# A first projection over successive tokens, and what is moved into its time, in a Hymba-style block on one Trainium2 core

## The chip, the core and the metric

The kernel runs on one core of one Trainium2 chip. The core has a matrix engine (TensorE, PE in the rows of the profile, with the weight loads apart as PEld), a vector engine (VectorE, DVE), a scalar engine (ScalarE, ACT), GpSimd (POOL) and SyncE (SP), which in this kernel issues nearly all DMAs. Each engine works through its own queue in order and waits on semaphores for the others. The metric is the device time of one execution in microseconds (us): 2374.28 us before the change, the median of 3 runs (2373.72 to 2376.62).

## What is computed

One layer of a streaming encoder trunk, batch 1, 2048 tokens of 1024 features, all float32. One RMSNorm feeds one projection, whose columns go to two mixers; both outputs are normalised, joined, projected and added to the input; a SwiGLU feed-forward layer follows. In short:

```python
h = rmsnorm(x, norm_mix_g)
u, q, k, v = split(h @ w_in)                  # 512 columns for u, 3 * 512 for q, k, v
# mixer A: 32 groups of 16 channels, one 64-state complex diagonal SSM per group
lam_bar = exp(lam * dt); b_bar = ((lam_bar - 1) / lam)[..., None] * b
s_t = lam_bar * s_{t-1} + b_bar u_t           # over the 2048 tokens
ya = gelu(Re(c s_t) + d * u_t); ya = ya * sigmoid(ya @ w_glu + b_glu)
# mixer B: 8 heads of 64, each chunk of 64 tokens sees itself and 8 chunks before it
yb = softmax(q k^T / 8 + rel_bias) v
x = x + concat(rmsnorm(ya), rmsnorm(yb)) @ w_out
x = x + (silu(hf @ w_gate) * (hf @ w_up)) @ w_down,  hf = rmsnorm(x)
out = rmsnorm(x)
```

## The kernel before, in words

Every product of float32 matrices is made of three matmuls (`mm3`, the matmul itself at L75): each operand is split into a high part (a cast on ACT) and a low part (a subtraction on DVE or POOL), and high times high, low times high and high times low are added up in PSUM. The PE's instructions stay in the order in which the program writes them (`Ordered`, `keep_in_program_order`); the order on the other engines and on SP's queue is set by a scheduler that goes by priorities, and is fixed when the program is built.

**First projection** (`u_phase`, L388 to 500). It makes `u`, 512 features by 2048 tokens, in four blocks `b` of 512 tokens. The tokens are taken by residue: token t is 8c + j, and a block holds two residues j with all 256 values of c, from an input `xp` that lies in that order. A block is four groups `f` of 128 features, each a sum over the inner dimension of 1024 in eight tiles `q`. Block 0 runs with q outermost over four PSUM banks, so it can follow its operands as they arrive; blocks 1 to 3 run group by group (`group`), each group through all q. `prep` loads and splits the operands of a block, `sums` loads the tokens again for the sums of squares and makes their inverse roots on DVE (`newton`, 14 small operations on 128x4), `spread_` turns these on the PE into a factor per token (tile `pb`), and `evac` (L448, tile `us`) multiplies the PSUM banks with it on DVE and stores the result to `u` in DRAM, laid out `[512, 8, 256]`: channel, residue, c. Between blocks `step` runs pieces of `ssm_prologue` (L155 to 386), which makes the SSM's matrices from its parameters: powers `pr`, `pi` (DVE), the powers `a8` (POOL), the products `v` and `wt` of powers with C and B (`cmul`, L280 to 282; DVE), `kt`, and transposes `bst` on the PE.

**Attention and SSM** (`att_phase`, from L620). `hT_unit(0)` loads the first 512 tokens (`xt`, 8 DMAs), scales them and splits them into `hi` and `lo` (L663 to 665), the operands of the first q, k and v products (`pf`). Then 128 steps follow, in which score blocks `sc`, transposes `pt` and products with v run, and between them pieces of eight `ssm_unit`s (L497 to 595), 64 channels each. A unit starts every 15 steps. It loads its `U` (128 x 4 x 256: residue and channel of the group by group by c) from `u`, and its matrices `Bst`, `Tm` and `Vm`; the PE first makes `pj<-U,Bst` (8 passes), POOL and DVE run the recurrence, and at the end the PE makes `pj<-U,Tm` and the rest of the output, which 8 DMAs store as `y`. `U` has one buffer, so the loads of a unit wait for the last read by the unit before it. The loads of a unit are issued from L506:

```python
for j in range(L):
    load(U[j * CH : (j + 1) * CH], S["u"][b * F : (b + 1) * F, j, :].rearrange("(g c) t -> c g t", c=CH))
```

Each of the 8 is 16 partitions by 4 groups by 256 values of c, 64 KB in runs of 1024 bytes. They all go through SP's queue, as do the stores of `y` and the other loads of the attention.

After the attention come the output projection (`mix`), the feed-forward layer (`gate_up`, `down`) and the last norm, which the change doesn't touch.

Of the kernel before, what the change touches and what calls it, by code (L numbers as in the profile page):

```python
# [13 lines left out]
ALU = mybir.AluOpType  # L14
# [29 lines left out]
PRO = 5  # L44
# [110 lines left out]
def ssm_prologue(k, ident, S):  # L155
# [3 lines left out]
    with tc.tile_pool(name="pro", bufs=1) as p:  # L159
# [158 lines left out]
        extend(pr, pi, 4, 4)  # L318
        a8 = S["a8"]
# [12 lines left out]
        def pc(a, qs, n):  # L332
            return a[:, qs, :n].unsqueeze(3).to_broadcast([P, 4, n, CH])

        def rc(a, qs):
            return a[:, qs, L - 1 :: -1].unsqueeze(3).to_broadcast([P, 4, L, CH])

        def cc(a, qs, n):
            return a[:, qs].unsqueeze(2).to_broadcast([P, 4, n, CH])

        for g2 in range(2):
            for c, bt in ((0, bbr), (1, bbi)):
                nc.gpsimd.dma_start(S["bb"][:, g2, c].rearrange("q n m -> n q m"), bt[g2 * NS : (g2 + 1) * NS])
        wts = []
        for b_ in range(4):
            qs = slice(4 * b_, 4 * b_ + 4)
            vt = [k.t(p, f"v{i}", [P, 4, 9, CH], bufs=2) for i in range(2)]
            cmul(vt[0][:], vt[1][:], pc(pr, qs, 9), pc(pi, qs, 9), cc(cr, qs, 9), cc(ci, qs, 9), [4, 9, CH], neg=True)
            for g2 in range(2):
                for c in range(2):  # L350
                    nc.gpsimd.dma_start(S["v"][qs, g2, c].rearrange("q n m -> n q m"),
                                      vt[c][g2 * NS : (g2 + 1) * NS].rearrange("n q k c -> n q (k c)"))
            if b_:
                yield
        for b_ in range(4):
            qs = slice(4 * b_, 4 * b_ + 4)
            wt = [k.t(p, f"wt{i}", [P, 4, L, CH], bufs=4) for i in range(2)]
            cmul(wt[0][:], wt[1][:], rc(pr, qs), rc(pi, qs), cc(bbr, qs, L), cc(bbi, qs, L), [4, L, CH])
            wts.append(wt)
        kt = k.t(p, "kt", [CH, 8, P], bufs=2)  # L360
        nc.gpsimd.memset(kt[:], 0.0)
        for b_ in range(4):
            nc.gpsimd.dma_start(S["kt"][:, 8 * b_ : 8 * b_ + 8, 0], kt[:])
        bb = k.t(p, "bbg", [P, NG, CH])
        nc.sync.dma_start(bb[:], S["bb"].rearrange("q g c n m -> (c n) (q g) m"))
        dm = k.t(p, "dm", [CH, NG, CH])
        V.tensor_tensor(dm[:], ident[:CH, :CH].unsqueeze(1).to_broadcast([CH, NG, CH]),
                        ddt[:].unsqueeze(2).to_broadcast([CH, NG, CH]), op=ALU.mult)
        vgs = []
        for b_ in range(4):  # L370
            vgs.append(k.t(p, "vg" if b_ < 2 else "bst", [P, 8, P], bufs=2))
            nc.sync.dma_start(vgs[b_][:], S["v"].rearrange("q g c n m -> (c n) (q g) m")[:, 8 * b_ : 8 * b_ + 8, :P])
        for b_ in range(4):
            gs = slice(8 * b_, 8 * b_ + 8)
            vg = vgs[b_]
            kt = k.t(p, "kt", [CH, 8, P], bufs=2)
            if b_ == 0:
                yield
# [6 lines left out]
            V.tensor_tensor(kt[:, :, :CH], kt[:, :, :CH], dm[:, gs], op=ALU.add)  # L385
            nc.gpsimd.dma_start(S["kt"][:, gs, 1], kt[:])
# [4 lines left out]
def u_phase(k, ident, S):  # L391

    tc, nc, io = k.tc, k.nc, k.io
    with ExitStack() as cx:
        p2 = cx.enter_context(tc.tile_pool(name="u2", side="right", bufs=2))
        p1 = cx.enter_context(tc.tile_pool(name="u1", side="right", bufs=1))
        p3 = cx.enter_context(tc.tile_pool(name="u3", side="right", bufs=4))
        psum = cx.enter_context(tc.tile_pool(name="ups", bufs=6, space=bass.MemoryType.PSUM, reuse_waits="tile"))
        psum2 = cx.enter_context(tc.tile_pool(name="ups2", bufs=2, space=bass.MemoryType.PSUM, reuse_waits="tile"))
        k.pro_psum = psum2  # L400
        wh, wl = k.t(p1, "wuh", [P, KT, DS], F32R), k.t(p1, "wul", [P, KT, DS], F32R)
        rsn = S["rsn"][:].rearrange("p (c j) -> p j c", j=L)
        te = k.te
        X, ST, pbs = {}, {}, {}

        def prep(b, each=None):
            X[b] = []
            for q in range(KT):
                if b == 0:
                    if q % 2 == 0:  # L410
                        xn = k.t(p2, "xn", [P, D], bufs=3)
                    raw = xn[:, q % 2 * DS : q % 2 * DS + DS]
                    nc.sync.dma_start(raw, io["w_u"][q * P : (q + 1) * P, :])
                    nc.scalar.activation(wh[:, q, :], raw, AF.Copy, scale=k.gm[:, q : q + 1])
                    nc.vector.scalar_tensor_tensor(wl[:, q, :], raw, k.gm[:, q : q + 1], f32(wh[:, q, :]),
                                                   op0=ALU.mult, op1=ALU.subtract)
                xt = k.t(p3, "xt", [P, 512])
                nc.sync.dma_start(xt[:], io["xp"][q * P : (q + 1) * P, 2 * b : 2 * b + 2, :].rearrange("p j c -> p (j c)"))
                hi, lo = k.t(p2, f"hi{q}", [P, 512], F32R), k.t(p2, f"lo{q}", [P, 512], F32R)
                nc.scalar.copy(hi[:], xt[:])  # L420
                nc.vector.tensor_tensor(lo[:], xt[:], f32(hi[:]), op=ALU.subtract)
                X[b].append((hi, lo))
                if each:
                    each(q)
            ST[b] = ss = k.t(p2, "ss", [P, 4])
            for i in range(4):
                xn = k.t(p2, "xn", [P, D], bufs=3)
                nc.sync.dma_start(xn[:], io["x"].rearrange("(h p j) d -> j h p d", p=P, j=L)[2 * b + i // 2, i % 2])
                nc.scalar.activation(xn[:], xn[:], AF.Square, accum_out=ss[:, i : i + 1])

        def mm(b, f, ps, q):
            fs = slice(f * P, (f + 1) * P)
            mm3(te, ps[:], wh[:, q, fs], wl[:, q, fs], X[b][q][0][:], X[b][q][1][:], q == 0, q == KT - 1)

        def sums(b):
            with tc.high_priority():
                ST[b] = newton(k, p2, ST[b][:], D, 4)

        def spread_(b):
            ps = k.t(psum2, "pp", [P, 512])  # L440
            spread(k, te, ps, ST[b], 0)
            pbs[b] = pb = k.t(p1, "pb", [P, 512])
            nc.scalar.copy(pb[:], ps[:])
            nc.scalar.copy(rsn[:, 2 * b : 2 * b + 2, :], pb[:].rearrange("p (j c) -> p j c", j=2))

        def evac(b, f, ps):
            us = k.t(p3, "us", [P, 2, NC], bufs=2)
            nc.vector.tensor_tensor(us[:], ps[:].rearrange("p (j c) -> p j c", j=2), pbs[b][:].rearrange("p (j c) -> p j c", j=2), op=ALU.mult)  # L448
            nc.sync.dma_start(S["u"][f * P : (f + 1) * P, 2 * b : 2 * b + 2, :], us[:])

        def group(b, f):
            ps = k.t(psum, "ps", [P, 512])
            for q in range(KT):
                mm(b, f, ps, q)
            return ps

        def finish(b, pss):
            with tc.high_priority():
                spread_(b)
                for f in range(4):  # L460
                    evac(b, f, pss[f])

        pss = [k.t(psum, "ps", [P, 512]) for _ in range(4)]

        def first(q):
            for f in range(4):
                mm(0, f, pss[f], q)
# [3 lines left out]
        def step(late=0):  # L471
            with tc.high_priority(offset=-late):
                next(pro)

        next(pro)
        prep(0, first)
        step(LATER)
        sums(0)
        held = pss
        for b in range(1, 4):  # L480
            prep(b)
            step()
            if b == 2:
                corner = k.t(p1, "corner", [64, 64])
# [4 lines left out]
            now = [group(b, 0)]  # L489
            finish(b - 1, held)  # L490
            now += [group(b, 1), group(b, 2)]
            sums(b)
            held = now + [group(b, 3)]
        step()
        finish(3, held)
# [3 lines left out]
def ssm_unit(k, p, psum, S, b, eng):  # L499
# [10 lines left out]
    for j in range(L):  # L510
        load(U[j * CH : (j + 1) * CH], S["u"][b * F : (b + 1) * F, j, :].rearrange("(g c) t -> c g t", c=CH))
# [108 lines left out]
def att_phase(k, ident, S, pro):  # L620
    tc, nc, io = k.tc, k.nc, k.io
    with ExitStack() as cx:
        aw = tc.alloc_tile_pool(name="aw", reuse_waits="tile", bufs=1, side="right")
        pfs = cx.enter_context(tc.tile_pool(name="apf", bufs=2, space=bass.MemoryType.PSUM, reuse_waits="tile"))
# [1003 lines left out]
```

## Time and profile before

| what | value |
|---|---|
| median of 3 runs | 2374.28 us (2373.72 to 2376.62) |
| span of the profiled execution, first to last instruction | 2370.8 us |
| PE busy | 2212.0 us (93%) |
| DVE, ACT, POOL busy | 1475.0, 1002.4, 1128.4 us (62, 42, 48%) |
| mean granted clock of the PE | 0.965 |
| first scores of the attention on the PE | at 178.83 us |
| loads of `U` | 64 DMAs of 64 KB, first issue at 192.9 us, last at 683.2 us |

The profiled execution is shown by its span alone; no time of its own is given beside it, so what lies around the span is seen only from the runs: their median is 3.5 us above it. A row of the timeline reads: start and duration in us, engine, line, operation, tile written <- tiles read, shape, and in brackets how long the engine stood idle before it and what released it. `SPq` rows are DMA issues on SP's queue: their duration is that of the issue, not of the transfer.

### The profile page before, as it was taken

The numbers are of one execution on the slowest core, as the hardware profiler recorded it, in microseconds if no ns is written. First come the engines' busy times: TensorE is split into PE (matmuls) and PEld (weight loads), VectorE is DVE, ScalarE is ACT, GpSimd is POOL, SyncE is SP. The second block draws the span as 40 slices with busy tenths as digits, with TensorE's granted clock in tenths as the row PEclk, the third lists the DMA queues.
The fourth block names the chain that finished last, engine by engine and source line by source line (L and its number), as shares of the span: only waits on it lengthen the run. The fifth ranks groups of instructions, "written<-read, shape, count | busy, mean of one in ns | idle before, by whom it ended". The sixth has DMA issues, their size and how long they took to land.

```text
span 2370.8 us, 30760 instructions
## 1 busy us (share of the span) xinstructions
PE 2212.0 (93%) x10712; PEld 1860.2 (78%) x10712; DVE 1475.0 (62%) x2247; ACT 1002.4 (42%) x1675; POOL 1128.4 (48%) x1268
## 2 busy tenths in 40 slices
PE   8588889999997899989999999999999989999996
PEld 6467778898986788768888887788888868888886
DVE  7644555756555855755776767766745365578675
ACT  5144545555556642243333334433333343345332
POOL 2313545656442333375555557655555464345442
PEclk9788999999998999989999999999999989999998
DMA  8587776766655334752544546654523187565541
GB/s 270 174 287 247 230 220 182 245 199 198 184 150 158 129 120 146 251 168 92 204 156 155 200 165 241 212 191 156 180 87 123 61 315 258 176 207 185 207 173 72
DMA packets 215220, 437.02 MB, mean 184 GB/s; under 512 B 27225, under 2 KB 57993, under 8 KB 207961
## 3 DMA queue, kind: packets, MB, share of 16 engines
q1 hardware_dynamic: 211480, 425.08, 54.1%
q0 software_dynamic: 3584, 9.98, 1.5%
q8 instruction: 84, 1.38, 0.2%
q14 instruction: 72, 0.58, 0.1%
HBM read 294.98 MB, written 132.15 MB: 180 GB/s over the span
## 4 chain that ended last, share of the span: by engine, by line
PE 50%; DVE 3%; issue 1%; POOL 1%; DMA 1%; ACT 1%; DVEq 0%; SPq 0%; ACTq 0%; POOLq 0%
PE X L75 19%; PE ps L75 17%; PE Y L75 10%; PE W L75 5%; DVE sa L1476 1%; DVE lo L152 1%; POOL c L152 0%; DVE hd L152 0%; DMA hd<-wc 0%; DVE S L1295 0%; DVE acc L1493 0%; DMA hd<-hq 0%; DVE g L1360 0%; DMA lo<-hc 0%; ACT hd L151 0%
## 5 line engine op out<-in xcount | busy, mean ns | idle before, releaser
L75 PE MATMUL X<-hi,c 128*128 128x512 f32 x1408 | 451.3, 391 | 8.0 <-ACT c L151 3.3
L75 PE MATMUL ps<-hd,hd 128*128 128x512 f32 (+1 forms) x1968 | 435.0, 384 | 7.7 <-DVE hd L152 4.6
L75 PEld LDWEIGHTS ps<-hd,hd 128*128 128x128 f32 x1968 | 361.5, 191 | 79.9 <-DVE hd L152 5.1
L152 POOL TENSOR_TENSOR c<-S,c 128x512 fp32r<-128x512 f32 x176 | 250.8, 1426 | 244.8 <-ACT c L151 242.9
L75 PEld LDWEIGHTS X<-hi,c 128*128 128x128 f32 x1408 | 265.6, 189 | 65.8 <-ACT c L151 3.7
L152 POOL TENSOR_TENSOR hd<-hd 128x1536 fp32r<-128x1536 f32 (+1 forms) x53 | 188.2, 3557 | 210.7 <-ACT hd L151 183.1
L75 PE MATMUL X<-lo,c 128*128 128x512 f32 x704 | 274.9, 390 | 0.0
L152 POOL TENSOR_TENSOR c<-raw,c 128x512 fp32r<-128x512 f32 x132 | 188.5, 1428 | 132.0 <-ACT c L151 102.8
L151 ACT CAST hd<-hd 128x1536 fp32r<-128x1536 f32 (+1 forms) x106 | 147.3, 1392 | 227.1 <-DMA hd<-hq 165.1
L75 PE MATMUL Y<-hi,c 128*128 128x512 f32 x704 | 229.4, 396 | 11.7 <-DVE u L1317 11.7
L1441 DVE TENSOR_TENSOR acc<-acc,ps 128x512 f32<-128x512 f32 x196 | 129.4, 682 | 90.6 <-PE ps L75 90.4
L75 PEld LDWEIGHTS Y<-hi,c 128*128 128x128 f32 x704 | 135.1, 192 | 41.7 <-DVE u L1317 13.3
L75 PE MATMUL pf<-hi,w 128*128 128x512 f32 x416 | 153.3, 418 | 14.3 <-ACT hi L664 10.5
L75 PE MATMUL big<-m,woh 128*128 128x512 f32 x512 | 161.9, 398 | 0.2 <-ACT woh L151 0.2
L544 POOL TENSOR_TENSOR st<-X,a 128x128 f32<-128x128 f32 (+2 forms) x136 | 46.8, 344 | 237.5 <-ACT X L530 227.5
L151 ACT CAST c<-S 128x512 fp32r<-128x512 f32 x176 | 109.2, 621 | 112.0 <-PE Y L75 59.1
L778 DVE CUSTOM_DVE_ANT_0 s<-sc,nb 128x640 f32<-128x640 f32 (+4 forms) x128 | 94.5, 738 | 98.3 <-PE sc L75 93.3
L75 PEld LDWEIGHTS X<-lo,c 128*128 128x128 f32 x704 | 132.9, 189 | 27.4
L1313 ACT COPY u<-X 128x512 f32<-128x512 f32 x132 | 77.0, 584 | 182.0 <-PE X L75 182.0
L151 ACT CAST c<-raw 128x512 fp32r<-128x512 f32 x132 | 82.1, 622 | 154.1 <-PE Y L75 82.9
L75 PE MATMUL Y<-lo,c 128*128 128x512 f32 x352 | 139.3, 396 | 0.0
L152 DVE TENSOR_TENSOR hd<-hd 128x1536 fp32r<-128x1536 f32 (+1 forms) x53 | 111.8, 2111 | 32.7 <-ACT hd L151 31.7
(376 smaller groups left out, 4724.3 us busy)
## 6 DMA issues: line engine op xcount, KB each, us to landing
w<-wss SPq DMA_DIRECT2D x36, 1024.0 KB, 5.7
hq<-g SPq DMA_DIRECT2D x140, 256.0 KB, 2.0
hd<-hq SPq DMA_DIRECT2D x42, 768.0 KB, 4.5
hd<-wc SPq DMA_DIRECT2D x42, 768.0 KB, 6.0
raw<-in_w_gate SPq DMA_DIRECT2D x44, 512.0 KB, 3.7
raw<-in_w_up SPq DMA_DIRECT2D x44, 512.0 KB, 4.1
wc<-px SPq DMA_DIRECT2D x66, 256.0 KB, 3.0
wss<-w SPq DMA_DIRECT2D x12, 1024.0 KB, 6.0
```

Source lines behind the costliest of these rows:

```text
L75: return self.tc.keep_in_program_order(self.tc.nc.tensor.matmul(*a, **b))
L151: nc.scalar.copy(hi, raw)
L152: (lo_eng or nc.gpsimd).tensor_tensor(lo, raw, f32(hi), op=ALU.subtract)
L544: eng.tensor_tensor(t[:, :, :, :n], src, ar, op=ALU.mult)
L778: nc.vector.tensor_tensor_reduce(s[:, :nk].rearrange("p (a b) -> p a b", a=nch), ps[:, :nch, :half], hd.nb[:, nk - 1 :: -1].rearrange("p ( ...
L1313: nc.scalar.copy(u[:], ps[:])
L1441: V.tensor_tensor(a, a, ps[:], op=ALU.add)
L1476: (nc.gpsimd if m else nc.vector).tensor_tensor(self.sa[m][:, :n], self.sa[m][:, :n], t[:, :n], op=ALU.add)
```

## The change

The first projection now takes 512 successive tokens to a block and runs every block with the inner dimension outermost, over hand-placed PSUM banks (`UBANKS`). The token tiles of block 0 are kept, and in its blocks 1 and 2 the phase makes from them the attention's first operands (`hT0`), so that `hT_unit(0)` and its 8 loads are gone. The prologue's pieces are handed out in another way: of the eight pairs of products `v` and `wt`, two stay on DVE and six go to POOL (tag "cq", 36 operations of 576 or 512 values), ahead of the powers `a8`. The layout of `u` in DRAM becomes `[4, 512, 8, 64]`: block, channel, residue, c within the block. So the loads of `U` become four times as many, each a fourth in size: 32 DMAs of 16 KB to a unit, in runs of 256 bytes.

```diff
-PRO = 5
+PRO = 2
+UX = 3
 def ssm_prologue
-            w = 576 if eng is V else 64
+            w = {"cm": 576, "cp": 64, "cq": 576}[tag]
...
+            cmul(vt[0][:], vt[1][:], pc(pr, qs, 9), pc(pi, qs, 9), cc(cr, qs, 9), cc(ci, qs, 9), [4, 9, CH], neg=True, **({} if b_ < 2 else dict(eng=nc.gpsimd, tag="cq")))
...
+            cmul(wt[0], wt[1], rc(pr, qs), rc(pi, qs), cc(bbr, qs, L), cc(bbi, qs, L), [4, L, CH], eng=nc.gpsimd, tag="cq")
...
+UBANKS = (0, 1, 2, 3), (4, 5, 6, 0), (1, 2, 3, 4), (5, 6, 0, 1)
-def u_phase(k, ident, S):
+def u_phase(k, ident, S, aw, raw0, hT0):
...
+                xr = k.t(ux, "x4", [P, 2, 512], bufs=UX)
+                nc.sync.dma_start(xr[:], io["xt"][2 * r * P : (2 * r + 2) * P, b * SB : (b + 1) * SB].rearrange("(q p) t -> p q t", p=P))
+                split(k, w[:, 0], w[:, 1], xr[:], nc.vector)
...
+        def evac(b, pss):
+            with tc.high_priority():
+                for f, ps in enumerate(pss):
+                    us = k.t(ux, "us", [P, L, SB // L], bufs=2)
+                    v = "p (c j) -> p j c"
+                    nc.vector.tensor_tensor(us[:], ps[:].rearrange(v, j=L), S["rsn"][:, b * SB : (b + 1) * SB].rearrange(v, j=L), op=ALU.mult)
+                    nc.sync.dma_start(S["u"][b, f * P : (f + 1) * P], us[:])
...
+            for q in range(KT):
+                if b == 1 and q < 4:
+                    for f in range(3):
+                        mm(b, f, q, pss[f])
+                    if q == 1:
+                        roots(0)
+                        evac(0, held)
+                    if q == 3:
+                        for q_ in range(4):
+                            mm(b, 3, q_, pss[3])
+                    continue
+                for f in range(4):
+                    mm(b, f, q, pss[f])
+                if b and q == 5:
+                    roots(b)
+            if b:
+                evac(b, pss)
+            held = pss
+            if b in (1, 2):
+                hT0(4 * (b - 1), 4 * b)
 def ssm_unit
     for j in range(L):
-        load(U[j * CH : (j + 1) * CH], S["u"][b * F : (b + 1) * F, j, :].rearrange("(g c) t -> c g t", c=CH))
+        for g in range(GB):
+            load(U[j * CH : (j + 1) * CH, g].rearrange("c (s t) -> c s t", s=NSB), S["u"][:, b * F + g * CH : b * F + (g + 1) * CH, j, :].rearrange("s c t -> c s t"))
 def att_phase
+                nc.vector.scalar_tensor_tensor(xt[:], xt[:], k.gm[:, q : q + 1], S["rsn"][:, :SB], op0=ALU.mult, op1=ALU.mult)
+                split(k, hi[:], lo[:], xt[:], nc.gpsimd)
...
-        for _ in hT_unit(0):
-            pass
...
-            "u": k.t(dram, "u", [DS, L, NC]), "y": k.t(dram, "y", [DS, L, NC]),
+            "u": k.t(dram, "u", [NSB, DS, L, SB // L]), "y": k.t(dram, "y", [DS, L, NC]),
```

(`UX` is the number of buffers for `x4`, `PRO` the number of pieces of the prologue that are left for the start of the attention.)

SP's queue at the start of unit 1, before the change: the first load of `U` stands ahead of the eight stores of unit 0's output, the other seven behind them, and the loads of `Tm` and `Vm` follow.

```order
L506 DMA U_2648<-u_64 16x4x256
L591 DMA y_65<-X_2580 16x4x256 x8
L506 DMA U_2648<-u_64 16x4x256 x7
L506 DMA Tm_2659<-kts_80 16x4x128 x8
L506 DMA Vm_2668<-vs_72 128x4x128
```

The same place after the change (L514 is the line of the unit's loads there).

```order
L514 DMA U_2550<-u_64 16x4x64
L600 DMA y_65<-X_2482 16x4x256 x8
L514 DMA U_2550<-u_64 16x4x64 x31
L514 DMA Tm_2585<-kts_80 16x4x128 x8
L514 DMA Vm_2594<-vs_72 128x4x128
```

Nothing else on the queue has moved here, but behind the stores stand 31 loads of `U` where 7 stood.

DVE's queue around the evacuation of block 0, before: `us` is the evacuation, `lo` the split of block 1's operands, and the rows on `nv`, `nf`, `no`, `ny` are the inverse roots of block 1 (`newton`), which have begun some rows earlier.

```order
L448 TENSOR_TENSOR us_831<-ps_125,pb_828 128x512
L104 CAST ny_895<-nf_894 128x4
L448 TENSOR_TENSOR us_834<-ps_126,pb_828 128x512
L107 TENSOR_TENSOR nf_894<-ny_895 128x4
L421 TENSOR_TENSOR lo_294_939<-xt_936,hi_293_938 128x512
L108 TENSOR_TENSOR nf_894<-nf_894,nv_893 128x4
L421 TENSOR_TENSOR lo_297_945<-xt_942,hi_296_944 128x512
```

The same place after: `us_747` and `us_750` are the first two evacuations of block 0, `hi0x` to `xt_202` (eight rows, of which the first and the last are shown) the attention's operands, `w` splits for blocks 1 and 2, `vw` the products `v` (twelve rows, of which one stands here), and `nv_641` begins the inverse roots of block 1.

```order
L449 TENSOR_TENSOR us_747<-ps_38_144,rsn_94 128x512
L449 TENSOR_TENSOR us_750<-ps_39_145,rsn_94 128x512
L646 SCALAR_TENSOR_TENSOR hi0x_151<-hi0x_151,g_mix_88,rsn_94 128x512
...
L646 SCALAR_TENSOR_TENSOR xt_202<-xt_202,g_mix_88,rsn_94 128x512
L153 TENSOR_TENSOR w_623<-x_206_624,w_623 128x1024
L153 TENSOR_TENSOR w_879<-x_263_880,w_879 128x1024
...
L283 TENSOR_TENSOR vw_223_676<-cm_226_682,cm_227_683 128x576
L449 TENSOR_TENSOR us_753<-ps_40_146,rsn_94 128x512
L449 TENSOR_TENSOR us_756<-ps_41_147,rsn_94 128x512
L102 TENSOR_SCALAR nv_641<-ss_628 128x4
```

The inverse roots of block 1, which ran between the evacuations of block 0, now stand behind both pairs of them and behind 22 other operations of 512 to 1024 values. On the PE, 54 matmuls stand between the spread of block 0's roots and that of block 1's.

More of the change, by code (lines that the diff above doesn't have):

```diff
@@ new lines, in u_phase, with prep @@
+        X, ST = {}, {}
+        def prep(b, r):
+            w = k.t(aw, "w", [P, 2, 2, 512], F32R, bufs=WB)
+            X[b, r] = w
+            qs = slice(2 * r, 2 * r + 2)
+            if b == 0:
+                wr = k.t(ux, "x4", [P, 2, DS], bufs=UX)
+                nc.sync.dma_start(wr[:], io["w_u"][2 * r * P : (2 * r + 2) * P, :].rearrange("(q p) f -> p q f", p=P))
+                for m in range(2):
+                    q = 2 * r + m
+                    raw = raw0(q)
+                    nc.sync.dma_start(raw[:], io["xt"][q * P : (q + 1) * P, :SB])
+                    g = k.gm[:, q : q + 1]
+                    nc.scalar.activation(wh[:, q, :], wr[:, m], AF.Copy, scale=g)
+                    nc.vector.scalar_tensor_tensor(wl[:, q, :], wr[:, m], g, f32(wh[:, q, :]), op0=ALU.mult, op1=ALU.subtract)
+                    split(k, w[:, 0, m], w[:, 1, m], raw[:], nc.vector)
+            else:
+                xr = k.t(ux, "x4", [P, 2, 512], bufs=UX)
+                nc.sync.dma_start(xr[:], io["xt"][2 * r * P : (2 * r + 2) * P, b * SB : (b + 1) * SB].rearrange("(q p) t -> p q t", p=P))
+                split(k, w[:, 0], w[:, 1], xr[:], nc.vector)
@@ L435, in sums @@
[L435 to L467, printed above, removed]
+            with tc.high_priority():
+                ST[b] = newton(k, ux, ss[:], D, 4)
@@ new lines, in roots @@
+        def roots(b):
+            with tc.high_priority():
+                ps = k.t(psum2, "pp", [P, 512])
+                spread(k, te, ps, ST[b], 0)
+                nc.scalar.copy(S["rsn"][:, b * SB : (b + 1) * SB], ps[:])
+        def evac(b, pss):
+            with tc.high_priority():
+                for f, ps in enumerate(pss):
[3 more added lines that the diff above has]
+                    nc.sync.dma_start(S["u"][b, f * P : (f + 1) * P], us[:])
@@ L469, in u_phase, with mm, step @@
+        def mm(b, f, q, ps):
+            fs = slice(f * P, (f + 1) * P)
+            x = X[b, q // 2]
+            mm3(te, ps[:], wh[:, q, fs], wl[:, q, fs], x[:, 0, q % 2], x[:, 1, q % 2], q == 0, q == KT - 1)
         pro = ssm_prologue(k, ident, S)
-        def step(late=0):
+        def step(n=1, late=0):
             with tc.high_priority(offset=-late):
-                next(pro)
+                for _ in range(n):
+                    next(pro)
         next(pro)
-        prep(0, first)
@@ L477, in u_phase @@
[L477 to L484, printed above, removed]
+        held = None
+        for b in range(NSB):
+            pss = [k.t(psum, f"ps{n}", [P, 512]) for n in UBANKS[b]]
+            for r in range(KT // 2):
+                prep(b, r)
+            sums(b)
+            if b == 0:
+                step(1, LATER)
+            elif b == 1:
+                step(4, LATER)
+            elif b == 2:
+                step(4, LATER)
+                corner = k.t(ux, "corner", [64, 64])
```

139 lines of the change are left out of this document (59 added, 80 removed).

## The prediction

> **What bounds the kernel now.** I read the profile's page first, then the waits of the PE in the first 200 us, then the timelines of SP's queue and of the PE at the start of each SSM unit, since the diff touches just these two stages.
>
> ```profile
> span 2370.8 us, 30760 instructions
> ...
> PE   8588889999997899989999999999999989999996
> ...
> PE 50%; DVE 3%; issue 1%; POOL 1%; DMA 1%; ACT 1%; DVEq 0%; SPq 0%; ACTq 0%; POOLq 0%
> ```
>
> Each digit is a slice of 59 us, in tenths. The PE is the bound nearly everywhere: 9 from slice 7 on, with a dip at slices 13 and 14, and half of the chain that ended last is the PE's own work. The PE's queue is in program order, so whatever the PE waits for adds to the end, unless a later wait shrinks by it. Only two stretches have gaps to win: the first three slices, and the seams of the attention.
>
> ```profile
> PE ps L75 <- DVE us L448: 19.3, 2, 10.7
> PE ps L75 <- ACT hi L420: 6.7, 3, 4.6
> PE pf L75 <- ACT hi L664: 5.8, 1, 5.8
> ...
> PE pp L75 <- DVE us L448: 2.7, 1, 2.7
> ```
>
> These are the PE's waits from 20 to 200 us (total, times, longest). The evacuation `us`, the splits `hi` of the projection and those of `hT_unit(0)` together make 19.3 + 6.7 + 5.8 + 2.7 = 34.5 us. That is what the change can take away at the front.
>
> **The loads of U, 64 turned into 256.** The profile's rows of SP's queue, one line for each SSM unit's loads (start, duration of the group's issues, count):
>
> ```profile
> 192.93 4.78 SPq L506 DMA_DIRECT2D U<-u  x8
> ...
> 264.99 4.49 SPq L591 DMA_DIRECT2D y<-X  x8
> 269.53 3.23 SPq L506 DMA_DIRECT2D U<-u  x7
> ...
> 339.75 3.35 SPq L506 DMA_DIRECT2D U<-u  x7
> ...
> 404.59 4.34 SPq L506 DMA_DIRECT2D U<-u  x7
> ...
> 475.05 5.03 SPq L506 DMA_DIRECT2D U<-u  x8
> ...
> 542.79 3.97 SPq L506 DMA_DIRECT2D U<-u  x8
> ...
> 610.25 3.23 SPq L506 DMA_DIRECT2D U<-u  x7
> ...
> 679.89 3.73 SPq L506 DMA_DIRECT2D U<-u  x7
> ```
>
> And the PE's first use of each of them:
>
> ```profile
> 207.98 1.89 PE L75 MATMUL pj<-U,Bst 128*128 128x256 f32 x8
> ...
> 274.74 1.97 PE L75 MATMUL pj<-U,Bst 128*128 128x256 f32 x8
> ...
> 347.14 1.97 PE L75 MATMUL pj<-U,Bst 128*128 128x256 f32 x8 [1.89 <-DMA Tm<-kts]
> ...
> 410.91 1.97 PE L75 MATMUL pj<-U,Bst 128*128 128x256 f32 x8 [1.48 <-DMA U<-u]
> ...
> 484.23 1.89 PE L75 MATMUL pj<-U,Bst 128*128 128x256 f32 x8
> ...
> 549.08 1.97 PE L75 MATMUL pj<-U,Bst 128*128 128x256 f32 x8
> ...
> 618.01 1.89 PE L75 MATMUL pj<-U,Bst 128*128 128x256 f32 x8
> ...
> 686.20 2.81 PE L75 MATMUL pj<-U,Bst 128*128 128x256 f32 x8 [3.52 <-DMA Tm<-kts]
> ```
>
> For units 1 to 7 the loads are just in time, or late: the last issue of U ends at 272.76, 343.10, 408.93, 480.08, 546.76, 613.48 and 683.62 us, and the PE begins 1.98, 4.04, 1.98, 4.15, 2.32, 4.53 and 2.58 us behind it, 21.6 us in all, three times after a wait. A load can't be issued earlier: U has one buffer, whose last reader is the unit before, and the eight stores of `y`, which wait for the end of the same unit, stand ahead on the queue. A landing needs most of that margin:
>
> ```profile
> DMA to landing us min/median/max: 2.1/2.5/5.4
> ```
>
> After the change the same place holds 24 more issues. The groups above give 3.23/7 = 0.46, 3.35/7 = 0.48, 3.97/8 = 0.50, 3.73/7 = 0.53, 4.34/7 = 0.62 and 5.03/8 = 0.63 us each. No row shows an issue of 16 KB; the count of runs in one (16 by 4) is the same as now, so I take the cost of an issue as set by the issue and not by its bytes, at 0.48 us, near the lower groups. That is 24 x 0.48 = 11.5 us to a unit. With a landing of 2.3 us behind the last issue, the last U is late by 7 x (11.5 + 2.3) - 21.6 = **75 us** over seven units. The first group's passes wait only for the 29th load, so the passes could begin 3 x 0.48 = 1.4 us sooner, -10 us in all. Bounds: at 0.33 us an issue (shorter than any group), 7 x (7.9 + 2.3) - 21.6 = 50 us; at 0.62, 7 x (14.9 + 2.3) - 21.6 = 99 us; both less the 10. For unit 0 the last issue ends at 197.71 and the PE comes at 207.98, 8 us behind the landing; 24 more at 0.48 to 0.60 take 11.5 to 14.4 us, so 0 to 6 us is lost there, as the front shifts; I take 2. What stands behind the U loads on SP (`Tm`, `Vm`, weights, `nb`, keys) comes 11 us later too, but the PE, waiting at `pj<-U,Bst`, has lost the same time by then.
>
> The Trainium skill's page "DMA: Bandwidth & Descriptors" (section "Bandwidth") speaks against this edit: transfers under 64 KB are, by its rule, dominated by descriptors, and its section on the anatomy of a DMA fits each with about 2.0 us fixed and the bytes on top. By that fit, an estimate if the fixed parts ran one behind the other, the 24 would cost 48 us to a unit and over 300 us in all; the rows above, eight loads in 3.97 us, show that they overlap, so I don't follow it.
>
> **The clock behind a long wait.** A wait of some 9 us does more than idle. In the trace the longest wait of this stretch ends at 82.57 us; the granted clock after it (PE busy, then clock) and the matmuls, first then and then in full run:
>
> ```profile
> 82.50:84.00 1.50, 1.43 (x4) 0.50 1.00 197
> 84.00:86.00 2.00, 2.00 (x6) 0.50 0.86 274
> 86.00:88.00 2.00, 2.00 (x9) 0.90 0.97 292
> ```
>
> ```profile
> 83.56 0.63 PE L75 MATMUL ps<-hi,wul 128*128 128x512 f32 x1
> 83.98 0.63 PE L75 MATMUL ps<-hi,wuh 128*128 128x512 f32 x1
> ```
>
> ```profile
> 55.09 0.39 PE L75 MATMUL ps<-hi,wuh 128*128 128x512 f32 x1
> 55.32 0.39 PE L75 MATMUL ps<-lo,wuh 128*128 128x512 f32 x1
> ```
>
> One matmul takes 0.42 us there and 0.23 us in full run, for about 3.6 us, so each long wait loses a further 1.7 us: 7 x 1.7 = **12 us**. The waits of 1.89 and 1.48 us above did not slow the passes behind them (1.97 us as elsewhere); the one of 3.52 us did (2.81 us).
>
> **The front, to 190 us.** Of the 34.5 us I take all as gone: q outermost lets blocks follow their operands, seven banks replace six, and hT(0) is made early. What comes new is mainly a wait at the spread of block 1's roots. By the order, the PE has 54 matmuls between the spreads of block 0 and block 1, 54 x 0.23 = 12.4 us, while DVE must first do four evacuations, eight scalings for hT(0), two splits of 1024, twelve products of 576 and `newton`:
>
> ```profile
> L448 DVE TENSOR_TENSOR us<-ps,pb 128x512 f32<-128x512 f32 x16 | 10.6, 683 | 17.7 <-ACT pb L443 15.7 <-DMA u<-us 2.0
> L152 DVE TENSOR_TENSOR w<-raw,w 128x1024 fp32r<-128x1024 f32 x5 | 6.1, 1222 | 11.1 <-ACT w L151 11.1
> L282 DVE TENSOR_TENSOR v<-cm,cm 128x576 f32<-128x576 f32 x8 | 6.1, 757 | 9.5 <-DMA vs<-v 9.4
> ```
>
> ```profile
> 127.28 0.17 DVE L101 TENSOR_SCALAR nv<-ss 128x4 f32<-128x4 f32 x1 [1.77 <-ACT xn L429]
> ...
> 130.76 0.16 DVE L109 SCALAR_TENSOR_TENSOR no<-nf,ny 128x4 f32<-128x4 f32 x1
> ...
> 158.76 0.73 DVE L663 SCALAR_TENSOR_TENSOR lo1x<-lo1x,g_mix,rsn 128x512 f32<-128x512 f32 x1
> 159.43 1.76 DVE L663 SCALAR_TENSOR_TENSOR hi2x<-hi2x,g_mix,rsn 128x512 f32<-128x512 f32 x1
> ```
>
> 4 x 0.68 + 8 x 0.73 + 2 x 1.22 + 12 x 0.76 + 3.6 (127.28 to 130.92) = 23.7 us, 11.3 more than the PE has. Next to POOL's subtraction of the same size,
>
> ```profile
> 160.61 1.72 POOL L665 TENSOR_TENSOR lo<-lo1x,hi 128x512 fp32r<-128x512 f32 x1
> ```
>
> a scaling took 1.76 us in place of 0.73. Eight such subtractions run on POOL in that stretch now; if each delays one operation by 1.03 us, the wait is 19.5 us. I take 17. The evacuations of the last block stand behind splits on DVE before `kt`'s products can use the PSUM bank: 0 to 11 us (four evacuations, four splits, some scalings), taken at 8; the spreads and splits of blocks 2 and 3 at 5 (0 to 8). New waits then are about 30 us, so the front gains 34.5 - 30 = **about 5 us**, between 23 gained (11.3 alone) and 4 lost. The six pairs of products on POOL, 36 operations of that size, are 62 us at 1.72 us each. They start once the powers are made, which is when the first evacuations run, and their results are due at the transposes ahead of the first scores, some 100 us later, so I cost them at nothing: the projection's matmuls hide them. Were DVE to hold POOL up by half as much again, the transposes would be late by 0 to 10 us.
>
> By the Trainium skill's page "SBUF — State Buffer" (section "Who interferes with whom") DVE and GpSimd share a pair of ports under an exclusive lock for a whole instruction, so a DVE operation with two inputs from SBUF blocks GpSimd's reads and is blocked by them. The 1.76 us row agrees. Taken strictly, an estimate, all of POOL's work in that stretch would be added to DVE's, some 27 us of wait where I take 17, and the sum would be 10 us higher; the upper end holds that.
>
> **Sum.** Span 2370.8 + 75 - 10 + 12 + 2 - 5 = 2444.8 us. The profile gives only the span; the median of the runs is 3.5 us above it, so the time is 2374.3 + 74 = **2448 us**.
>
> **Rivals.** (a) *Faster.* An issue of 16 KB could be far cheaper than one of 64 KB, if what paces the queue is bytes rather than issues: then 32 small ones take the time of eight large ones and the front alone counts, 2374 - 23 = 2351 us. It decides where 7 x (24s + 2.3) - 21.6 falls under 23, that is below s = 0.17 us an issue. Against it: loads of 64 KB go out at 0.46 us and so do other sizes; no group lies below. (b) *The change does not pay at the front, and the loads are hidden:* 2374 + 4 to 20 us from locked DVE and POOL, about 2388; it needs the same cheap issue, but the contention too. (c) *Dear issues:* at 0.62 us, with unit 0 late by 6 and the front at +4: 2374 + 99 - 10 + 12 + 6 + 4 = 2485, with the strict lock 2495. (d) *Nothing:* front and loads cancel at s near 0.17; there is no reason for it.
>
> **How the numbers follow.** My forecast, U loads late in seven units, has a chance of 0.84, of which 0.80 within the range; (a) 0.07, (b) 0.03, (c) beyond the range 0.04, (d) 0.02. The low end is 0.33 us an issue and the best front: 2374 + 50 - 10 + 12 - 23 = 2403, the high end (c) at 2485; I set 2405 to 2487. About 0.2%, 5 us, is what a measurement of this kernel can tell from no change. Faster 0.07, same 0.02, slower 0.91.
>
> **What would show it.** Right: SP's rows with 31 loads of U lasting some 15 us behind each group of stores, and the PE idle 8 to 11 us before `pj<-U,Bst` in units 1 to 7, released by U, at clock 0.50 behind it; a wait of 10 to 20 us at the spread of block 1's roots, released by `newton`'s last row on DVE; first scores within 15 us of 178.8. Wrong: U's group no longer than some 6 us, or PE waits at `pj<-U,Bst` of under 4 us; or first scores earlier than 160 us.

## The result, and the profile after

The changed kernel takes 2453.18 us, the median of 4 runs (2452.14 to 2457.17), against 2375.45 us of the kernel before on the same chip (median of 4): a ratio of 1.0329 by the runs' means, with a 95% interval of 1.031 to 1.0348. The forecast was 2448 us, within 2405 to 2487. The profiled execution has a span of 2450.2 us, 79.4 us more than before.

The page of the changed kernel, with the parts that answer to those shown of before:

```profile
span 2450.2 us, 30897 instructions
...
PE   7668779788988789998999999899999989999996
...
PE 72%; DMA 8%; DVE 7%; SPq 4%; POOL 3%; issue 3%; ACT 2%; DVEq 0%; ACTq 0%; POOLq 0%
```

The digits of the first twelve slices, which are the projection and the attention, have fallen from mostly 8 and 9 to mostly 7 and 8; from slice 20 on hardly anything has changed. In the chain that ended last, DMA now has 8% and SP's queue 4%, where they had 1% and nothing.

The waits of the PE from 20 to 205 us, then from 205 to 860 us (total, times, longest):

```profile
PE pp L76 <- DVE no L110: 25.9, 2, 22.2
PE pp L76 <- issue: 13.0, 1, 13.0
PE pp L79 <- ACT bst L291: 5.6, 3, 4.5
PE sc L76 <- DVE mn L802: 3.7, 1, 3.7
PE ps L76 <- DVE us L449: 2.3, 1, 2.3
```

```profile
PE pj L76 <- DMA U<-u: 66.5, 7, 12.1
PE pt L79 <- DVE ptl L821: 11.9, 9, 2.0
```

One row, `pj` waiting for U, holds 66.5 us in seven waits. The first scores come at 185.14 us, 6.3 us later than before. So the front lost 6.3 us and everything behind it 79.4 - 6.3 = 73.1 us.

The start of unit 1 on SP's queue of the changed kernel, and on the PE:

```profile
268.97 4.96 SPq L600 DMA_DIRECT2D y<-X  x8
273.97 14.48 SPq L514 DMA_DIRECT2D U<-u  x31
288.49 3.70 SPq L514 DMA_DIRECT2D Tm<-kts  x8
```

```profile
288.55 3.44 PE L76 MATMUL pj<-U,Bst 128*128 128x256 f32 x8 [9.94 <-DMA U<-u]
...
446.77 3.75 PE L76 MATMUL pj<-U,Bst 128*128 128x256 f32 x8 [10.28 <-DMA U<-u]
```

31 issues take 14.48 us, 0.47 us each, behind the stores of `y`, and the PE begins as they end, having waited 9.94 us. Its eight passes then take 3.44 us in place of 1.97. The windows of the PE around this wait say why (from and to, length, PE busy and its matmuls, granted clock, then the DMA engines' busy share and GB/s):

```profile
278.60:288.50 9.90, 0.01 (x1) 0.64 0.16 35
288.55:290.50 1.95, 1.95 (x5) 0.50 0.26 51
290.50:292.50 2.00, 2.00 (x11) 0.74 0.37 74
292.50:294.50 2.00, 2.00 (x11) 1.00 0.57 127
```

The PE runs nothing for 9.9 us, and for some 3 us behind it the clock stands at half; by these rows 0.50 x 1.95 + 0.26 x 2.00 = 1.5 us are lost to it at this unit.

### The profile page after: what moved, and what is told of

Same layout as the page of the kernel before. It is cut to its first block, busy times and chain, and to the rows that moved or that the text cites. A ratio compares the mean times of both kernels' runs of the same rounds, so it can differ in the third digit from the quotient of the medians.

```text
span 2450.2 us, 30897 instructions
## 1 busy us (share of the span) xinstructions
PE 2222.0 (91%) x10712; PEld 1871.2 (76%) x10712; DVE 1480.3 (60%) x2198; ACT 998.0 (41%) x1659; POOL 1185.5 (48%) x1308
## 4 chain that ended last, share of the span: by engine, by line
PE 72%; DMA 8%; DVE 7%; SPq 4%; POOL 3%; issue 3%; ACT 2%; DVEq 0%; ACTq 0%; POOLq 0%
PE X L76 18%; PE ps L76 18%; PE Y L76 9%; PE pf L76 8%; PE big L76 7%; PE W L76 5%; PE pj L76 4%; SPq L514 3%; PE sc L76 2%; PE pt L79 2%; DMA xt<-in_xt 1%; DMA raw<-in_x 1%; DMA lo<-hc 1%; DMA w<-wss 1%; DVE lo L153 1%
```

## The experiments

Two questions were put: whether the 73 us are the issues of the U loads, and not their bytes, their short runs or the new order of the tokens; and what made the front 6 us longer where a gain of 5 was forecast. This table has what each run's profile gives: the first scores, the rest of the span behind them, and the waits at `pj<-U,Bst`, with the ratio to the kernel before (95% interval).

| kernel | first scores, us | rest, us | waits for U, us | ratio |
|---|---|---|---|---|
| before | 178.83 | 2192.0 | 6.9 | 1 |
| changed | 185.14 | 2265.1 | 66.5 | 1.0329 (1.031 to 1.0348) |
| e1: changed, 8 big loads | 193.93 | 2195.9 | 7.8 | 1.0067 (1.0042 to 1.0092) |
| e2: before, 32 loads, short runs | 177.10 | 2282.3 | 79.0 | 1.0339 (1.0317 to 1.036) |
| e3: before, 32 loads, long runs | 177.24 | 2268.2 | 63.0 | 1.0272 (1.0247 to 1.0297) |
| g5: before, 16 loads | 177.76 | 2224.9 | 25.3 | 1.01 (1.0061 to 1.0139) |
| f1: before, 1 load | 187.15 | 2202.7 | none | 1.0041 (1.0028 to 1.0055) |
| f2: changed, loads on two queues | 186.63 | 2240.7 | 3.8 | 1.0211 (1.0193 to 1.0228) |
| g4: changed, `lo` on DVE | 183.22 | 2269.2 | 63.1 | one run, 2454.25 us |
| e4: e1, sums first | 180.28 | 2194.9 | 6.0 | 1.0012 (0.9997 to 1.0028) |
| f3: e1, sums between | 176.10 | 2195.0 | 8.4 | 0.9986 (0.9976 to 0.9996) |
| f4: f3, 1 load | 222.37 | 2200.7 | none | 1.0188 (1.0173 to 1.0204) |
| g1: f3, stores of u from ACT | 187.67 | 2192.5 | 7.6 | 1.0032 (1.0017 to 1.0046) |

(In e2 and e3 3 us of the waits are at unit 0. A wait counts here whether the profile names `U` or `Tm` as its end, since the passes read U and `Bst` alone.)

**e1: the layout of u and the loads of before, in the changed kernel.**

```diff
-            "u": k.t(dram, "u", [NSB, DS, L, SB // L])
+            "u": k.t(dram, "u", [DS, L, NC])
-                    nc.sync.dma_start(S["u"][b, f * P : (f + 1) * P], us[:])
+                    nc.sync.dma_start(S["u"][f * P : (f + 1) * P, :, b * (SB // L) : (b + 1) * (SB // L)], us[:])
     for j in range(L):
-        for g in range(GB):
-            load(U[j * CH : (j + 1) * CH, g].rearrange("c (s t) -> c s t", s=NSB), S["u"][:, b * F + g * CH : b * F + (g + 1) * CH, j, :].rearrange("s c t -> c s t"))
+        load(U[j * CH : (j + 1) * CH], S["u"][b * F : (b + 1) * F, j, :].rearrange("(g c) t -> c g t", c=CH))
```

> The changed kernel with one part undone: u lies in DRAM as before, so a unit loads U by 8 DMAs of 64 KB again, and the projection's stores carry the short runs of 256 bytes instead. Theory (issues on SP's queue): the waits at pj<-U,Bst, 66.5 us in the changed kernel, fall to 5 to 9 us, and with the clock lost behind them the time falls by 65 to 78 us, to 2375 to 2388 us; the front stays as it is (first scores near 185 us). Rival (the front, or the successive tokens, cost the time): the time stays above 2430 us.

2392.57 us. The waits for U fell to 7.8 us and the rest of the span to 2195.9 us, 69 us under the changed kernel and 4 above before: the loads account for what was lost behind the first scores. The time missed the expected 2388 us by 5, because the front grew by 9 us more: its wait for block 1's roots is 39.2 us here. The stores of u, now in 1024 runs of 256 bytes, are slower to issue, as the profile's rows for the tile `us` show (durations of an issue in ns, min, median, max):

```profile
L450 SPq DMA_DIRECT2D u<-us x16: 512/528/1981, 45.2 to 160.1; - x16
```

In the changed kernel the median is 327 ns. That is small beside 39.2 us. What weighs more is the order on the queue: here the last of block 1's four loads for the sums of squares has come to stand behind the second pair of them on SP, and so behind the evacuations:

```profile
73.50 1.49 SPq L450 DMA_DIRECT2D u<-us  x2
75.08 0.61 SPq L433 DMA_DIRECT2D raw<-in_x  x1
```

In the changed kernel that load went out at 46.83 us, with the first pair.

**e2 and e3: 32 loads to a unit in the kernel before, once with short and once with long runs.** e2 cuts each load along c, into pieces of 16x4x64 with runs of 256 bytes:

```diff
     for j in range(L):
-        load(U[j * CH : (j + 1) * CH], S["u"][b * F : (b + 1) * F, j, :].rearrange("(g c) t -> c g t", c=CH))
+        for s in range(4):
+            load(U[j * CH : (j + 1) * CH, :, 64 * s : 64 * s + 64], S["u"][b * F : (b + 1) * F, j, 64 * s : 64 * s + 64].rearrange("(g c) t -> c g t", c=CH))
```

e3 cuts by group, into pieces of 16x256 with runs of 1024 bytes:

```diff
     for j in range(L):
-        load(U[j * CH : (j + 1) * CH], S["u"][b * F : (b + 1) * F, j, :].rearrange("(g c) t -> c g t", c=CH))
+        for g in range(GB):
+            load(U[j * CH : (j + 1) * CH, g], S["u"][b * F + g * CH : b * F + (g + 1) * CH, j, :])
```

> The kernel before with one thing changed: the 8 loads of U in a unit are cut into 32 along c, 16 KB each in runs of 256 bytes (16x4x64), as in the changed kernel. Theory: PE waits of 7 to 12 us at pj<-U,Bst in units 1 to 7, some 65 us in all, time 2440 to 2455 us. Rival (the front carries the loss): 2374 to 2385 us.

> The kernel before with the 8 loads of U in a unit cut into 32 by group: 16 KB each, but in runs of 1024 bytes as before (16x256). Theory (the count of issues): the same time as with the short runs, within 10 us of it, 2435 to 2455 us. Rival (the short runs of 256 bytes are what is slow): close to the kernel before, 2374 to 2385 us.

2458.53 and 2442.98 us, e2 3.5 us above its range and e3 within it. Splitting the loads alone, with nothing else of the change, gives the whole loss, and long runs take little of it away. The two differ by 15.6 us where at most 10 were expected. It is not the issues: SP's rows for unit 3 of e2, and then of e3, are

```profile
431.04 0.79 SPq L506 DMA_DIRECT2D U<-u  x2
435.74 14.89 SPq L506 DMA_DIRECT2D U<-u  x30
```

```profile
423.83 1.25 SPq L506 DMA_DIRECT2D U<-u  x3
428.88 14.66 SPq L506 DMA_DIRECT2D U<-u  x29
```

0.50 and 0.51 us each. What differs is what a pass has to wait for. Cut along c, each of the passes needs loads of all 32; cut by group, the first passes need only their own group's, the first of them without the last three issues, 1.5 us earlier, and in four of the seven units one load more goes out ahead of the stores of `y`. Over seven units that makes some 2 us each, the 79.0 against 63.0 us of waits. This is read from the rows; no run sets the cut apart from the length of the runs. The changed kernel cuts by group as well, and its waits of 66.5 us and rest of 2265.1 us are close to those of e3.

**g5: 16 loads to a unit in the kernel before** (as e2, with two pieces of 128 in place of four of 64).

> The kernel before with the 8 loads of U in a unit cut into 16 of 32 KB along c. By the prediction's sum, with 8 issues more to a unit: 7 x (8 x 0.48 + 2.3) - 21.6 = 21 us of added lateness, so waits of some 28 us in all at pj<-U,Bst with the 6.9 that are there, and a time 21 to 31 us above before, the upper part if the clock falls behind each wait (about 1.009 to 1.013). Rival (a threshold of size between 64 and 16 KB rather than a sum of issues): near before or near the 2440 to 2458 us of the 32 loads.

2402.03 us, 27 us above before, with 25.3 us of waits, as the sum of issues had it. 8, 16 and 32 loads give waits of 6.9, 25.3 and 79.0 us: no threshold, but a sum of issues, less the 2 us or so of slack that some units have. The rest of the span grew by 32.9 us, 18.4 of it waits; about 1.5 us for the clock at each of the five units whose passes took 3.4 to 3.75 us leaves some 7 us that these rows don't name.

**f1: one load to a unit in the kernel before**, with u in DRAM as residue, channel of the group, group, c.

```diff
-            nc.sync.dma_start(S["u"][f * P : (f + 1) * P, 2 * b : 2 * b + 2, :], us[:])
+            for j in range(2):
+                nc.sync.dma_start(S["u"][2 * b + j, :, 8 * f : 8 * f + 8].rearrange("c g t -> g c t"), us[:, j])
...
-    for j in range(L):
-        load(U[j * CH : (j + 1) * CH], S["u"][b * F : (b + 1) * F, j, :].rearrange("(g c) t -> c g t", c=CH))
+    load(U[:], S["u"].rearrange("j c g t -> (j c) g t")[:, GB * b : GB * b + GB])
```

> The kernel before with u laid out in DRAM by residue, channel of the group, group, c, so that a unit loads U by one DMA of 512 KB instead of 8 of 64 KB; the projection's stores become two each. Theory (issues on SP's queue): seven issues fewer to a unit, 7 x 0.48 = 3.4 us, of which a longer landing takes back 1 to 2 us; the three waits of 1.89, 1.48 and 3.52 us shrink, and the time falls by 3 to 8 us, to 0.9965 to 0.999 of before. Rival (the waits in the kernel before hang on something else): 0.999 to 1.003.

Slower, 2388.6 us: this expectation failed, and the time lies above the rival's range too. All waits for U are gone, so the mechanism is there, but 8.3 us are lost in the front, and the rest of the span is 10.7 us longer than before. In the front the stores of u have doubled, and an issue takes 574 ns in place of 327 (medians in the rows of `us`); the evacuations wait 6.1 us for them where they waited 2.0. That these stores are the whole 8.3 us is not shown. In the rest of the span the waits for transposed probabilities (`pt <- ptl`) have grown from 11.1 to 18.4 us and 6.8 us of waits for `X` on ACT are new. Why an earlier start of the units makes those longer was not tried; it stays open.

**f2: the changed kernel's 32 loads, two groups of four from ACT's queue.**

```diff
-    def load(out, in_):
-        ins = nc.sync.dma_start(out, in_)
+    def load(out, in_, q=nc.sync):
+        ins = q.dma_start(out, in_)
...
-            load(U[j * CH : (j + 1) * CH, g].rearrange("c (s t) -> c s t", s=NSB), S["u"][:, b * F + g * CH : b * F + (g + 1) * CH, j, :].rearrange("s c t -> c s t"))
+            load(U[j * CH : (j + 1) * CH, g].rearrange("c (s t) -> c s t", s=NSB), S["u"][:, b * F + g * CH : b * F + (g + 1) * CH, j, :].rearrange("s c t -> c s t"), nc.scalar if g % 2 else nc.sync)
```

> The changed kernel with the same 32 small loads of U, but half of them (two groups of four) issued from ACT's queue instead of SP's. Theory (what counts is the number of issues that follow one another on one queue): 16 issues on SP, 8 more than before, so the waits at pj<-U,Bst fall from 66.5 us to 15 to 35 us and the time to 2395 to 2425 us, unless ACT's own work is late behind its issues. Rival (the small DMAs themselves, wherever they are issued): 2445 to 2460 us.

2428.03 us. The same small DMAs, no fewer, cost 25 us less when half of them go out from another queue: it was the issues in a row on one queue, and the rival is out. The waits for U fall from 66.5 to 3.8 us, further than expected, while the time is 3 us above its range. For not all of that fall is a gain: ACT works in order too, its exponentials wait behind its issues, and the PE waits elsewhere (ACT's timeline):

```profile
279.29 6.63 ACTq L514 DMA_DIRECT2D U<-u  x14
286.31 0.61 ACT L805 ACTIVATE s<-s,mn 128x384 f32<-128x384 f32 x1 [5.98 <-DMA U<-u]
```

The waits at `pt <- ptl` rose from 11.9 to 37.9 us. In unit 1 the last issue of U on SP ends at 291.45 us, 3 us later than in the changed kernel, and the PE comes at 293.41 without a wait, since it had been held up before. The Trainium skill, "DMA: Bandwidth & Descriptors", section "Rules for kernel authors", says of spreading DMAs over SP, ACT and GpSimd that it doesn't help bandwidth and only saves the sequencer's issue time; here it was the issue time that was saved, and this run agrees.

**g4: the subtractions of hT0 on DVE, in the changed kernel.** `split(k, hi[:], lo[:], xt[:], nc.gpsimd)` becomes `nc.vector`. It tells whether POOL slows DVE in the stretch ahead of block 1's roots, where DVE's rows of the changed kernel read

```profile
47.63 0.74 DVE L646 SCALAR_TENSOR_TENSOR hi1x<-hi1x,g_mix,rsn 128x512 f32<-128x512 f32 x1
48.30 1.78 DVE L646 SCALAR_TENSOR_TENSOR lo1x<-lo1x,g_mix,rsn 128x512 f32<-128x512 f32 x1
```

> The changed kernel with one thing moved: the eight subtractions lo of hT0 run on DVE instead of POOL, in the same stretch ahead of block 1's newton. If POOL's subtractions delay DVE as the rows of the changed kernel suggest (some 8.2 us over that stretch), moving them costs 8 x 0.68 = 5.4 us and gives back 8.2, so the wait at the spread of block 1's roots goes from 22.2 to about 19 us. Rival (the long DVE rows have another cause): the 8 operations are simply added, and it goes to about 27 us.

The wait went to 20.31 us with eight operations more on DVE. The scalings and the splits of `w` all returned to their short times:

```profile
50.24 0.74 DVE L646 SCALAR_TENSOR_TENSOR lo1x<-lo1x,g_mix,rsn 128x512 f32<-128x512 f32 x1
...
51.57 1.22 DVE L153 TENSOR_TENSOR w<-x,w 128x1024 fp32r<-128x1024 f32 x1
```

So in this stretch POOL's subtractions did not unburden DVE; by this one profile DVE does them itself in less time than it loses beside them. From the first scaling to the evacuation behind the products `v` its rows take 22.7 us with them (46.45 to 69.11), and 26.3 us without (46.31 to 72.56).

**e4, f3: the sums of squares earlier, with big loads.** e4 calls `sums(b)` ahead of the operands of blocks 1 to 3; f3 puts it in their middle:

```diff
             for r in range(KT // 2):
                 prep(b, r)
-            sums(b)
+                if b and r == 1:
+                    sums(b)
+            if b == 0:
+                sums(b)
```

> As e1 (big loads), and in blocks 1 to 3 the loads and sums of squares come ahead of the operands, so that the inverse roots of block 1 stand on DVE ahead of the products v and among the scalings. Theory (the wait of 22.2 us at the spread of block 1's roots comes from DVE's queue ahead of newton): that wait falls under 8 us, and the time is 8 to 20 us under e1. Rival (DVE and POOL have a fixed amount of work up to the first scores, so the wait comes back later): within 5 us of e1.

> As e4 (big loads, early sums of squares), but the loads and sums of a block stand between the first and the second half of its operands, not ahead of them. Theory (e4's waits of 14.0 and 5.2 us for w come from operands queued behind the sums on SP): these two fall by 10 us or more together, the wait for newton stays under 10 us, first scores at 162 to 175 us and a time of 2360 to 2374 us, under the kernel before. Rival (the stores of u and DVE set the front, not the order of the loads): 2372 to 2385 us.

In e4 the wait for block 1's roots fell from 39.2 to 5.6 us, though no work was taken off DVE or POOL: newton now stands on DVE's queue among the scalings. A part came back as waits for casts of `w` (24.7 us with the 9.1 at the start, 14.0 of them at 110.76 us), but the time fell by 13 us, to 2379.49. In f3 the wait of 14.0 us did not go, against the expectation (15.61 us at 106.77), and the time, 2374.64 us, lies just past the end of the range and within the rival's; the first scores came 4.2 us earlier than in e4. SP's rows of f3 show what holds the operands `x` of block 2's second half and block 3:

```profile
75.25 10.14 SPq L450 DMA_DIRECT2D u<-us  x2
...
94.79 3.85 SPq L450 DMA_DIRECT2D u<-us  x2
98.69 2.38 SPq L426 DMA_DIRECT2D x<-in_xt  x2
```

Stores of u, which wait for evacuations, stand ahead of them. f3 is the one version that comes out below both kernels, by 0.14% (0.04 to 0.24%) under before, which is as good as the same.

**g1: those stores from ACT's queue.** In f3, `nc.sync.dma_start(S["u"]...)` becomes `nc.scalar.dma_start`.

> As f3 (big loads, sums between the operands), with the 16 stores of u issued from ACT's queue instead of SP's. Theory (f3's wait of 15.6 us for w comes from operand loads that stand on SP behind stores which wait for the evacuations): that wait goes, first scores at 158 to 170 us, time 2357 to 2370 us. Rival (ACT, now waiting for the evacuations itself, is late with its casts, or the loads wait for buffers anyway): 2370 to 2385 us.

The rival held. The wait of 15.6 us went, so the stores had held those operands up, but the PE now waits 12.43 us at the roots of block 1 for ACT, and 16.84 us ahead of `kt`'s products, where the profile names no releaser: ACT waits for evacuations in its turn (12.57 us at 87.45), and 2385.27 us is slower than f3.

**f4: f3 with one load to a unit**, u laid out as in f1 and eight stores to each evacuation.

> As f3, with u laid out as in f1: one load of 512 KB to a unit, and eight stores for each evacuation. If both the issues of a unit and the order of the loads count: f3's time less 3 to 8 us. Rival (128 stores on SP in the front delay the operands behind them): first scores 5 to 20 us later than in f3, and a time at or above f3's.

The rival held, by more than expected: 53.7 us of waits for casts of `w` in the front (24.6 in f3), first scores at 222.37 us, 2423.54 us. 128 stores on SP do to the operands of the projection what 32 loads did to U.

## Why the prediction was right

**The U loads.** This was the forecast's main term, and it was right in mechanism and size. Added lateness was put at 75 us less 10 for passes that begin early; the waits for U rose from 6.9 to 66.5 us, by 59.6. An issue was taken at 0.48 us from groups of 0.46 to 0.63, and with 16 KB it is 0.46 to 0.53, for short and long runs alike: that a load of 16 KB costs the queue as much as one of 64 KB was assumed, and e2 and e3 now show it. The landing fell to a median of 1.8 us from 2.5, which explains part of the 5 us that the term was too high. f2, which leaves the DMAs as they are and moves half of them to another queue, shows that the path was SP's issues, though only 25 us came back. The fixed 2.0 us to a DMA that the prediction quotes from the Trainium skill's page "DMA: Bandwidth & Descriptors" (section "Anatomy of one DMA") and sets aside was fitted there to DMAs issued from GpSimd, while these loads go out from SP. Whether two buffers for U would hide the issues was not tried.

**Unit 0** was put at 2 us lost; the PE reached it without a wait in the changed kernel, and waited 3.1 and 3.2 us in e2 and e3, where the front was not late.

**The clock** was put at 12 us. The stage lost 73.1 us, 59.6 of it waits; 13.5 us are left, and seven times the 1.5 us of the windows above is 10.5. That is right within what is left for other small waits. The waits themselves spread further than the 8 to 11 us that were to show the forecast right: 6.97 to 12.09 us.

**The front** had the wrong sign: 5 us gained were forecast, 6.3 lost were measured, 2 us outside the bounds that were given to it without the strict lock. The gain was real; the waits for `us`, `hi` and `pf<-hi` went but for 2.3 us at `us`. The step that failed is the sum of the new waits: 30 us were taken, and 44.5 came. Three terms were too small. First, the wait for block 1's roots was taken at 17 us, with 10 to 20 as the sign of being right, and is 22.2. It was worked out with evacuations at 0.68 us, but they now read PSUM and the factors in another order (`"p (c j) -> p j c"`) and take 1.10 us (profile's rows of `us`):

```profile
L449 DVE TENSOR_TENSOR us<-ps,rsn x16: 1054/1104/1177, 44.3 to 150.1; 128x512 f32<-128x512 f32 x16
```

and beside POOL not only five of the eight scalings were slow but also the two splits, 4.50 us in place of 2.4. The changed kernel's DVE rows for these splits, beside POOL's last two subtractions, are

```profile
56.79 4.50 DVE L153 TENSOR_TENSOR w<-x,w 128x1024 fp32r<-128x1024 f32 x2
```

The strict lock, by the Trainium skill's page "SBUF — State Buffer", section "Who interferes with whom", would have made the wait 27 us by the prediction's estimate; its own rows give 11.3 + 8 x 1.72 = 25.1. 22.2 lies between that and the 17 that were taken; the rows and g4 agree with the rule for operations of like size. Second, `kt`'s products were taken at 8 us and waited 13.0, from the end of block 3's last matmul at 138.28 us to 151.29, right behind the last evacuation. DVE's rows of this stretch:

```profile
137.71 1.41 DVE L687 SCALAR_TENSOR_TENSOR xt<-xt,g_mix,rsn 128x512 f32<-128x512 f32 x2
139.03 1.22 DVE L153 TENSOR_TENSOR w<-raw,w 128x1024 fp32r<-128x1024 f32 x1
140.17 2.03 DVE L449 TENSOR_TENSOR us<-ps,rsn 128x512 f32<-128x512 f32 x2
145.14 1.23 DVE L153 TENSOR_TENSOR w<-raw,w 128x1024 fp32r<-128x1024 f32 x1 [2.94 <-ACT w L152]
149.15 2.04 DVE L449 TENSOR_TENSOR us<-ps,rsn 128x512 f32<-128x512 f32 x2 [2.78 <-DMA u<-us]
```

Scalings and a split put the first evacuation off to 140.17 us, as the prediction had it. It did not have the 7 us between the second and the third: a split there waits for its weights, and behind it DVE still waits 2.78 us until the store of an earlier evacuation, issued at 141.25 us, gives back one of the two buffers of `us`. That is read from the rows; no run took it away. Third, the transposes `pp<-ident,vw` wait 5.6 us for the copies `bst`, which were taken as hidden; before the last two of these copies ACT itself waits for the stores of earlier ones (3.06 and 1.41 us). The products on POOL, costed at nothing, were hidden: POOL ended them at 136.7 us, 35 us before the transposes began. The other waits, taken at 5, are 3.7 at block 2's roots.

So 32.2 us went and 44.5 came, 12.3 us more of waits, of which 6.3 are seen: up to the first scores the PE was also busy 4.2 us less (127.7 in place of 131.9 us), and 2.2 us of short waits for `lo` went.

The total of 74 us came out at 79.4 because the terms that were right are the large ones, and in part by luck: the U loads were taken 5.4 us too high and the front 11.3 us too low, and these partly cancel. The order of the rivals was right as well: cheap issues (rival a) would have made the kernel faster only at under 0.17 us each, and no unit's group of 16 KB loads in the changed kernel, e2 or e3 lies under 0.46.

## What to carry to other kernels

Count the DMAs that stand on one queue between the event that frees a buffer and the first reader, and price each at the spacing that the trace shows for back-to-back issues, not at its bytes: cutting 8 loads into 32 moved the same bytes and cost 24 issues, some 11 us, to each unit. When a projection is turned round so that its output suits its own loop, look at who reads the output next, since the layout between the two is paid for by the stores or by the loads, here by the number of the loads. And before work is moved from DVE to POOL, check in the trace what the two cost each other side by side.

## What the runs showed of the hardware

- Issues on SP's queue are 0.46 to 0.53 us apart when some 30 follow one another, for loads of 16 KB in runs of 256 as of 1024 bytes. The stores of u differ by their layout: 327 ns for an issue in the kernel before and the changed one, 528 in e1 (1024 runs of 256 bytes), 574 in f1 (half the bytes, with the channels reordered).
- Every wait for U of 3.1 us or more left the eight passes behind it slow, at 2.8 to 3.8 us. Below that the length alone doesn't decide: 2.47 us (f3, unit 2) and 2.98 us (g1, unit 7) left them at 1.96 and 1.97 us, while after 2.44 us (g1, unit 2) they took 3.63 and after 1.99 us (f2, unit 7) 3.52, with the granted clock at 0.50 in both. What decides there stays open.
- An evacuation of 128x512 from PSUM takes 0.68 us in order and 1.10 us when both operands are read with a stride of eight.
